# Gate and up projections by seven block products in place of eight, in a decoder block on one core

## The chip, the cores and the metric

The kernel runs on one core of a Trainium2 chip. Its time is the device time of that core in microseconds, as the median of several runs.

## What is computed

One layer of a decoder trunk in float32: a mixer (short convolution, forgetting attention, sliding-window attention, merged by gates), cross attention into 256 memory tokens, a feed-forward, and a last RMSNorm. 512 tokens, 1024 features. The change is in the feed-forward, whose hidden width is 2816, and in what stands around it:

```python
def swiglu(xn, w_gate, w_up, w_down):
    return (jax.nn.silu(xn @ w_gate) * (xn @ w_up)) @ w_down

x = x + cross_attention(rms_norm(x, xattn_norm_g[l]), rms_norm(mem, mem_norm_g[l]), w_xq[l], w_xkv[l], w_xo[l])
x = x + swiglu(rms_norm(x, ffn_norm_g[l]), w_ffn_gate[l], w_ffn_up[l], w_ffn_down[l])
return rms_norm(x, final_norm_g)
```

## The kernel before

Activations lie feature-major, [feature, token]: a product is weights (stationary, 128 x 128) times activations (moving, 512 tokens). Each float32 operand goes to TensorE as a high part, rounded to float32r by ScalarE, and a low part, the difference, from VectorE. A product is then three matmuls (`mm3`: high x high, high x low, low x high), and each matmul loads its own weights.

All weights come as one stream of units of 128 x 1024 numbers (512 KB) in the order of use. `fetch` issues a unit's load on SP's queue into one of three raw buffers (`wr`); `prepare` splits it into one of three `wh` and three `wl` buffers; `next_unit` hands over unit i, having prepared up to i + 2 and asked for loads up to i + 4. `project` runs one unit: eight chunks of features by three matmuls, 24 in all, into a PSUM bank.

The stages near the change, in order:

- *xo*, the output projection of cross attention: for each of eight chunks c a unit of `w_xo`, and then `residual`, which adds the product to x1, splits x1 times the feed-forward's gain into `gx1h` and `gx1l`, and sums the squares for the norm (`add_square`, partly on GpSimd).
- *gate/up*: 22 column blocks j (two units each, one of gate, one of up, products `pfg` and `pfu`). The norm's 1/rms comes after the first two products (`rms_column`, `rms_row`; tiles `ssq_x`, `bc_x`) and is multiplied into both products by VectorE; ScalarE takes the Silu; the product of the two is split at once into `hdh` and `hdl`. Between the blocks 2 to 9, eight groups of four TensorE transposes (`x2T`) turn x1 token-major for the last residual, and ScalarE copies them to `x2t`.
- *down*: token-major, 22 units of `w_d`, eight accumulators (`acc`) of 128 tokens x 512 features. The last four units (`TAIL`) are held back, so that the token blocks finish one after the other and their last norm overlaps with matmuls.

The order of instructions on each engine is set by a scheduler when the program is built, and may differ from the order of the code; each engine then works in its order. A wait is for the last reader or writer of a buffer, by semaphores. Loads on SP's queue are issued in order, so one that waits for its buffer holds back those behind it. Numbers in names of tiles such as `wr119` are the unit's place in the weight stream.

Of the kernel before, what the change touches and what calls it, by code (L numbers as in the profile page):

```python
# [8 lines left out]
F32 = mybir.dt.float32  # L9
F32R = mybir.dt.float32r  # L10
# [6 lines left out]
P = 128  # L17
D = 1024
# [30 lines left out]
def trunk_kernel(ctx: ExitStack, tc: tile.TileContext, a, out: bass.AP):  # L49
    """Activations live feature-major ([feature, token]) so that every product is weights  # L50
    (stationary) x activations (moving); values, and the last projection, come token-major.

    A float32 operand x goes to TensorE as hi = x rounded to float32r and lo = x - hi, which
    is exact, in three one-pass products hi*hi + hi*lo + lo*hi.
    """
# [19 lines left out]
    def split(src, hi, lo, scale=None):  # L75
        """hi + lo = src * scale (scale: a number or one value for each partition)."""
# [9 lines left out]
    # ---------------------------------------------------------------- constants  # L86
# [14 lines left out]
    wlo = pool(ctx, "wlo", bufs=3)  # L101
    stream = []
    order = [("w_a", 25), ("w_g", KC), ("w_o", KC), ("w_k", KC), ("w_q", 2), ("w_v", 4), ("w_q", 6), ("w_v", 4)]
    done = {}
    for name, n in order + [("w_xo", KC), ("w_f", 2 * NF), ("w_d", NF)]:
        t = a[name][done.get(name, 0) :]
        done[name] = done.get(name, 0) + n
        if name == "w_g":
            for c in range(KC):
                stream += [("g", 3 * c + j, t[3 * c + j], 1024) for j in range(3)]  # L110
                stream += [("b", 2 * c + j, a["w_b"][2 * c + j], 768) for j in range(2)]
        else:
            stream += [(name, i, t[i], 1024) for i in range(n)]
    raws, parts = {}, {}
    cursor = [0, 0]

    def fetch(upto):
        while cursor[0] < min(upto, len(stream)):
            i = cursor[0]
            _, _, ap, n = stream[i]  # L120
            raws[i] = wraw.tile([P, 1024], F32, tag="wr", name=f"wr{i}")
            nc.sync.dma_start(raws[i][:, :n], ap)
            cursor[0] += 1

    def prepare(upto):
        while cursor[1] < min(upto, len(stream) - TAIL):
            i = cursor[1]
            n = stream[i][3]
            fetch(i + 1)
            hi = whi.tile([P, 1024], F32R, tag="wh", name=f"wh{i}")  # L130
            lo = wlo.tile([P, 1024], F32R, tag="wl", name=f"wl{i}")
            split(raws.pop(i)[:, :n], hi[:, :n], lo[:, :n])
# [5 lines left out]
    def next_unit(kind):  # L138
        i = used[0]
        assert stream[i][0] == kind, (stream[i][:2], kind)  # L140
# [17 lines left out]
    # two banks for products, in every phase  # L158
# [5 lines left out]
    def rms_column(acc, nblk, sb, name):  # L164
        """acc: squares summed over the chunks, [P, tokens] -> 1/rms as [token, block]."""
# [13 lines left out]
        # one Newton step, as the square root comes from a table  # L179
# [6 lines left out]
    def rms_row(rstd, nblk, sb, name, row=None):  # L186
        """[token, block] -> [P, tokens], the same on every partition."""
# [28 lines left out]
    # ================================================================ mixer  # L216
    x1, gxh, gxl = None, None, None

    def residual(ps, c, acc, g):
        nc.vector.tensor_tensor(x1[:, c, :], x1[:, c, :], ps, op=ALU.add)  # L220
        split(x1[:, c, :], gxh[:, c, :], gxl[:, c, :], gains[:, g, c : c + 1])
# [4 lines left out]
    with yo, mixer:  # L226
        # x times the norm's gain; 1/rms is multiplied in after the products
# [6 lines left out]
        with ExitStack() as attn:  # L234
# [42 lines left out]
            # -------- x, its norm, and [fox v | swa v | forget logits], token-major  # L277
            with ExitStack() as first:
# [22 lines left out]
                # keeps TensorE's clock up until the first loads are there  # L301
# [738 lines left out]
```

## Time and profile before

| | us |
|---|---|
| median of 3 runs | 1046.54 |
| the runs | 1046.53 to 1048.02 |
| span of the profiled execution | 1044.6 |
| TensorE busy | 1032.5 |
| VectorE busy | 547.5 |
| ScalarE busy | 401.6 |
| GpSimd busy | 62.5 |

The profiled execution has no time of its own beside its span: the result gives one time per run, and the span is 1.9 us under their median, for what lies ahead of the first instruction and behind the last. A group's row has line, engine, operation, output<-inputs, shapes and count, then busy time and mean ns of one, then the idle time ahead of them and what ended it. A recorded matmul's duration reaches from its start to its last result, so consecutive matmuls overlap, and their rate is read from their starts.

### The profile page before, as it was taken

To read this page: it belongs to the slowest core of one execution; us is meant where nothing else is said; L and a number is where in the kernel's file an instruction comes from. 1 tells how busy PE (TensorE), PEld (TensorE's weight loads), DVE (VectorE), ACT (ScalarE), POOL (GpSimd) and SP (SyncE) were. 2 spreads that over 40 slices of the span, in tenths; PEclk is the share of its full clock that TensorE was granted. 3 is DMA by queue.
4 is the path that set the end of the run, shared out by engine and by line. 5 is a ranking of instruction groups with operands and counts; after the bars stand their busy time and mean duration, and the time that the engine had idled before them with its cause. 6 is when DMAs were issued, how large, how long until landed. Compare 5 with 4: busy or idle time off the path is not lost.

```text
span 1044.6 us, 12547 instructions
## 1 busy us (share of the span) xinstructions
PE 1032.5 (99%) x4936; PEld 838.1 (80%) x4936; DVE 547.5 (52%) x915; ACT 401.6 (38%) x688; POOL 62.5 (6%) x62
## 2 busy tenths in 40 slices
PE   8999999999999999999999999999999999999997
PEld 6877777878888888888988888888888888888886
DVE  6557767677744444465746554454444444431224
ACT  6445454445522222354534443343333233221124
POOL 5100000001000000033100002200000000000000
PEclk9999999999999999999999999999999999999999
DMA  7431111112222322253442223222223323323222
GB/s 259 144 109 61 61 61 60 62 61 71 91 91 94 100 99 91 91 202 101 141 141 82 81 81 100 90 92 84 98 98 104 100 82 101 99 83 101 93 69 80
DMA packets 30363, 102.20 MB, mean 98 GB/s; under 512 B 3763, under 2 KB 4027, under 8 KB 30177
## 3 DMA queue, kind: packets, MB, share of 16 engines
q1 hardware_dynamic: 27648, 93.37, 27.2%
q0 software_dynamic: 1936, 6.98, 2.2%
q10 hardware_dynamic: 720, 1.07, 0.3%
q8 instruction: 38, 0.62, 0.2%
q14 instruction: 21, 0.16, 0.0%
HBM read 99.29 MB, written 3.68 MB: 99 GB/s over the span
## 4 chain that ended last, share of the span: by engine, by line
PE 97%; DMA 1%; DVE 1%; ACT 1%; issue 1%; SPq 0%; DVEq 0%; ACTq 0%
PE pg L71 4%; PE pg L73 4%; PE pg L72 4%; PE pfg L71 4%; PE pfg L73 4%; PE pfu L72 4%; PE pfu L73 4%; PE pfu L71 4%; PE pfg L72 4%; PE acc L71 4%; PE acc L73 4%; PE acc L72 4%; PE pc L71 2%; PE pbr L73 2%; PE pbr L72 2%; PE pbr L71 2%
## 5 line engine op out<-in xcount | busy, mean ns | idle before, releaser
L78 ACT CAST wh<-wr 128x1024 fp32r<-128x1024 f32 (+1 forms) x167 | 172.3, 1032 | 440.3 <-issue 129.9
L79 DVE TENSOR_TENSOR wl<-wr,wh 128x1024 fp32r<-128x1024 f32 (+1 forms) x167 | 200.0, 1199 | 104.0 <-ACT wh L78 103.3
L71 PE MATMUL pg<-hh,wh 128*128 128x512 f32 x192 | 76.3, 397 | 0.0
L73 PE MATMUL pg<-hh,wl 128*128 128x512 f32 x192 | 75.9, 395 | 0.0
L72 PE MATMUL pg<-hl,wh 128*128 128x512 f32 x192 | 75.9, 395 | 0.0
L71 PE MATMUL pfg<-gx1h,wh 128*128 128x512 f32 x176 | 70.4, 400 | 0.0
L71 PE MATMUL pfu<-gx1h,wh 128*128 128x512 f32 x176 | 69.6, 395 | 0.0
L72 PE MATMUL pfu<-gx1l,wh 128*128 128x512 f32 x176 | 69.6, 395 | 0.0
L73 PE MATMUL pfg<-gx1h,wl 128*128 128x512 f32 x176 | 69.6, 395 | 0.0
L72 PE MATMUL pfg<-gx1l,wh 128*128 128x512 f32 x176 | 69.6, 395 | 0.0
L73 PE MATMUL pfu<-gx1h,wl 128*128 128x512 f32 x176 | 69.6, 395 | 0.0
L73 PE MATMUL acc<-wh,hdl 128*128 128x512 f32 x144 | 57.1, 396 | 0.0
L72 PE MATMUL acc<-wl,hdh 128*128 128x512 f32 x144 | 57.1, 396 | 0.0
L71 PE MATMUL acc<-wh,hdh 128*128 128x512 f32 x144 | 57.1, 396 | 0.0
L640 DVE TENSOR_TENSOR g<-pg,rows 128x512 f32<-128x512 f32 x24 | 16.5, 689 | 76.2 <-PE pg L73 76.2
L841 DVE TENSOR_TENSOR tu<-pfu,row_x 128x512 f32<-128x512 f32 x22 | 15.2, 690 | 70.3 <-PE pfu L73 70.3
L211 POOL TENSOR_TENSOR acc_x<-acc_x,sq_acc_x 128x512 f32<-128x512 f32 x21 | 36.1, 1721 | 182.1 <-ACT sq_acc_x L210 181.7
L839 DVE TENSOR_TENSOR tg<-pfg,row_x 128x512 f32<-128x512 f32 x22 | 15.2, 690 | 53.9 <-PE pfg L73 51.1
L73 PEld LDWEIGHTS pg<-hh,wl 128*128 128x128 f32 x192 | 36.1, 188 | 8.7
L71 PEld LDWEIGHTS pg<-hh,wh 128*128 128x128 f32 x192 | 36.1, 188 | 8.5
L72 PEld LDWEIGHTS pg<-hl,wh 128*128 128x128 f32 x192 | 36.1, 188 | 8.4
L71 PE MATMUL pc<-hh,wh 128*128 128x512 f32 x96 | 41.6, 434 | 0.0
(390 smaller groups left out, 2325.7 us busy)
## 6 DMA issues: line engine op xcount, KB each, us to landing
wr<-in_w_f SPq DMA_DIRECT2D x44, 512.0 KB, 3.4
wr<-in_w_a SPq DMA_DIRECT2D x25, 512.0 KB, 3.5
wr<-in_w_g SPq DMA_DIRECT2D x24, 512.0 KB, 3.4
wr<-in_w_d SPq DMA_DIRECT2D x22, 512.0 KB, 3.4
wr<-in_w_b SPq DMA_DIRECT2D x16, 384.0 KB, 3.0
wr<-in_w_o SPq DMA_DIRECT2D x8, 512.0 KB, 3.5
wr<-in_w_k SPq DMA_DIRECT2D x8, 512.0 KB, 3.5
wr<-in_w_q SPq DMA_DIRECT2D x8, 512.0 KB, 3.4
```

Source lines behind the costliest of these rows:

```text
L71: nc.tensor.matmul(o, wh, xh, start=first, stop=False, **kw)
L72: nc.tensor.matmul(o, wh, xl, start=False, stop=False, **kw)
L73: nc.tensor.matmul(o, wl, xh, start=False, stop=last, **kw)
L78: nc.scalar.copy(hi, src)
L79: nc.vector.tensor_tensor(lo, src, f32(hi), op=ALU.subtract)
L211: nc.gpsimd.tensor_tensor(acc[:, :n], acc[:, :n], sq[:, :n], op=ALU.add)
L640: nc.vector.tensor_tensor(g, pg, row0, op=ALU.mult)
L839: nc.vector.tensor_tensor(tg, pg, row2, op=ALU.mult)
L841: nc.vector.tensor_tensor(tu, pu, row2, op=ALU.mult)
```

## The change

The feed-forward's gate and up weights are cut into blocks: for a pair of column blocks (n = 0, 1) and the even and odd chunks of features (e = 0, 1) the units a11, a12, a21, a22, each with four chunks of gate and four of up. The activations are cut into even and odd chunks and two halves of 256 tokens. A two-by-two block product takes eight block products; here seven are made, of sums of blocks (Winograd's form). Each product is one unit: 2 (gate, up) x 4 chunks x 3 = 24 matmuls of 256 columns. There are 11 pairs, so 77 products.

The seven units of a pair, in order, are a11; a21 + a22; the sum of the two before; a12; a21 + a11; the sum of the third and fourth; a22. Of the four sums, two are made by loading one block and adding the other over it with an accumulating DMA on GpSimd's queue (buffers `ws`, two), and two by VectorE (buffers `wt`, two). The sums of activations (`b1`, `b2`, `bt`) are made in the xo stage. Products gather in three PSUM tiles per pair (`pz`, `px`, `py`), and ScalarE and VectorE copy and combine them into `c1` and `c2`, from which come the gated activations `hd`, unsplit. 1/rms is multiplied into gate alone; the up side's is applied to the last additions, per token. The split of `hd` moves to the down stage (`hidden`), two units ahead of use. The transposes of x1 stand between gate/up and down.

```diff
+            for c in range(n):
+                a11, a12, a21, a22 = (t[4 * c + j] for j in range(4))
+                stream += [
+                    (name, a11, 1024),
+                    (name, (a21, a22), 1024),
+                    (name, (-1, -2), 1024),
+                    (name, a12, 1024),
+                    (name, (a21, a11), 1024),
+                    (name, (-3, -2), 1024),
+                    (name, a22, 1024),
+                ]
...
     def fetch(upto):
...
+            if not isinstance(ap, tuple):
+                if held_by["wr"] == 3:
+                    return
+                raws[i] = wraw.tile([P, 1024], F32, tag="wr", name=f"wr{i}")
+                nc.sync.dma_start(raws[i][:, :n], ap)
+                held_by["wr"] += 1
+            elif not is_local(ap):
+                if held_by["ws"] == 2:
+                    return
+                raws[i] = wsum[0].tile([P, 1024], F32, tag="ws", name=f"ws{i}")
+                nc.sync.dma_start(raws[i], ap[0])
+                nc.gpsimd.dma_start(raws[i], ap[1], accum_op=ALU.add)
+                held_by["ws"] += 1
...
     def prepare(upto):
...
+            if is_local(ap):
+                raws[i] = wsum[0].tile([P, 1024], F32, tag="wt", name=f"wt{i}")
+                nc.vector.tensor_tensor(raws[i], read(i + ap[0]), read(i + ap[1]), op=ALU.add)
...
     def next_unit(kind):
...
         prepare(i + 3)
-        fetch(i + 5)
+        fetch(i + (7 if kind == "w_f" else 5))
...
-        split(x1[:, c, :], gxh[:, c, :], gxl[:, c, :], gains[:, g, c : c + 1])
...
+            nc.scalar.activation(flat, x1[:, c, :], AF.Copy, scale=gains[:, G_FFN, c : c + 1])
+            if e == 0:
+                nc.vector.tensor_tensor(tt[:, 0, :], gx[:, 0, 0, :], gx[:, 0, 1, :], op=ALU.subtract)
+                split(gx[:, 0, 0, :], b1[0][:, q, 0, :], b1[1][:, q, 0, :], -1.0)
+                split(tt[:, 0, :], bt[0][:, q, 0, :], bt[1][:, q, 0, :])
+            else:
+                nc.vector.tensor_tensor(tt[:, 1, :], gx[:, 1, 1, :], tt[:, 0, :], op=ALU.add)
+                split(tt[:, 1, :], bt[0][:, q, 1, :], bt[1][:, q, 1, :])
+                nc.vector.tensor_tensor(tt[:, 2, :], gx[:, 0, 1, :], gx[:, 1, 1, :], op=ALU.subtract)
+                nc.vector.tensor_tensor(tt[:, 3, :], gx[:, 1, 0, :], tt[:, 1, :], op=ALU.subtract)
+                split(gx[:, 1], b2[0][:, q], b2[1][:, q])
+                split(tt[:, 2:4, :], bt[0][:, q, 2:4, :], bt[1][:, q, 2:4, :])
...
-            project(pg, "w_f", gxh, gxl)
-            project(pu, "w_f", gxh, gxl)
...
+        def product(ps, x, j, first):
+
+            wh, wl = next_unit("w_f")
+            for u in range(2):
+                o = ps[:, u * H : (u + 1) * H]
+                for q in range(KC // 2):
+                    w = slice((4 * u + q) * P, (4 * u + q + 1) * P)
+                    mm3(
+                        o, wh[:, w], wl[:, w], x[0][:, q, j, :], x[1][:, q, j, :],
+                        first and u == 0 and q == 0, q == KC // 2 - 1, skip=True,
+                    )
...
+            product(pz, b1, 0, True)
+            nc.scalar.copy(c1[:, 0], gu(pz))
+            product(px, bt, 0, True)
+            nc.scalar.copy(m5, gu(px))
+            product(pz, bt, 1, False)
+            nc.scalar.copy(c1[:, 1], gu(pz))
...
+            product(py, b2, 0, True)
+            nc.vector.tensor_tensor(c1[:, 0], gu(py), c1[:, 0], op=ALU.subtract)
+            product(pz, bt, 2, False)
+            nc.scalar.copy(c2[:, 1], gu(pz))
+            nc.vector.tensor_tensor(c2[:, 1], c2[:, 1], m5, op=ALU.subtract)
+            product(px, b2, 1, False)
+            nc.vector.tensor_tensor(c1[:, 1], gu(px), c1[:, 1], op=ALU.subtract)
+            product(pz, bt, 3, False)
+            nc.scalar.copy(c2[:, 0], gu(pz))
+            for n, cc in enumerate((c1, c2)):
...
+                nc.vector.tensor_tensor(cc[:, :, 0, :], cc[:, :, 0, :], r, op=ALU.mult)
+                nc.scalar.activation(cc[:, :, 0, :], cc[:, :, 0, :], AF.Silu)
+
+                nc.vector.tensor_tensor(h, cc[:, :, 1, :], cc[:, :, 0, :], op=ALU.mult)
...
+        def hidden(f):
...
+            split(hd[:, f, :], hh, hl)
...
             wh, wl = next_unit("w_d")
+            if f + 2 < NF - TAIL:
+                hidden(f + 2)
...
-                nc.vector.tensor_tensor(zt[:, c], o, base, op=ALU.add)
+                nc.vector.scalar_tensor_tensor(
+                    zt[:, c], o, r2[:, t : t + 1], base, op0=ALU.mult, op1=ALU.add
+                )
```

VectorE before, in the middle of gate/up (`tg`, `tu` are gate and up times 1/rms, `hdl` the low part of the gated product); one column block of the feed-forward is six rows:

```order
L841 TENSOR_TENSOR tu13_6880<-pfu13_6818,row_x2_5919 128x512
L842 TENSOR_TENSOR tu13_6880<-tu13_6880,tg13_6879 128x512
L79 TENSOR_TENSOR wl135_6890<-wr135_6823,wh135_6889 128x1024
L79 TENSOR_TENSOR hdl_5816<-tu13_6880,hdh_5815 128x512
L839 TENSOR_TENSOR tg14_6949<-pfg14_6887,row_x2_5919 128x512
L79 TENSOR_TENSOR wl136_6920<-wr136_6853,wh136_6919 128x1024
```

VectorE in the changed kernel, from the second pair (units 112 to 118) towards the third (119 to 125); `wl116` and `wl117` are the low parts of the second pair's fifth and sixth units, `ws120` is the third pair's first accumulated sum:

```order
L195 TENSOR_TENSOR wt121_6398<-ws120_6234,wr119_6203 128x1024
L90 TENSOR_TENSOR wl116_6231<-ws116_6097,wh116_6230 128x1024
L90 TENSOR_TENSOR wl117_6265<-wt117_6262,wh117_6264 128x1024
L195 TENSOR_TENSOR wt124_6494<-wt121_6398,wr122_6297 128x1024
L953 TENSOR_TENSOR c1_1_6163<-py1_6162,c1_1_6163 128x512
L90 TENSOR_TENSOR wl118_6294<-wr118_6172,wh118_6293 128x1024
L90 TENSOR_TENSOR wl119_6326<-wr119_6203,wh119_6325 128x1024
L956 TENSOR_TENSOR c2_1_6164<-c2_1_6164,m5_1_6165 128x512
L958 TENSOR_TENSOR c1_1_6163<-px1_6161,c1_1_6163 128x512
L964 TENSOR_TENSOR c1_1_6163<-c1_1_6163,row_x2_6028 128x2x256
L90 TENSOR_TENSOR wl120_6358<-ws120_6234,wh120_6357 128x1024
```

The scheduler has moved the third pair's sums `wt121` and `wt124` ahead of the second pair's fifth and seventh low parts (`wl116`, `wl118`).

SP's queue of loads before, in gate/up, one plain load per unit:

```order
L122 DMA wr114_6035<-in_w_f 128x1024
L122 DMA wr115_6081<-in_w_f 128x1024
L122 DMA wr116_6111<-in_w_f 128x1024
L122 DMA wr117_6157<-in_w_f 128x1024
L122 DMA wr118_6187<-in_w_f 128x1024
```

SP's queue in the changed kernel, the third pair's loads; for each `ws` an accumulating DMA (`L171`) of the same size stands in GpSimd's queue, which waits until the plain load has landed:

```order
L164 DMA wr119_6203<-in_w_f 128x1024
L170 DMA ws120_6234<-in_w_f 128x1024
L164 DMA wr122_6297<-in_w_f 128x1024
L170 DMA ws123_6329<-in_w_f 128x1024
L164 DMA wr125_6404<-in_w_f 128x1024
```

Five loads on SP and two on GpSimd take the place of four on SP per pair of column blocks; the load of `ws120` waits for the last reader of `ws113`, which is its low part `wl113`.

ScalarE before, where gate/up ends and down begins (`hdh` is the high part of the last gated product, `wh151` on are units of `w_d`):

```order
L840 ACTIVATE tg21_7439<-tg21_7439 128x512
L78 CAST wh151_7470<-wr151_7383 128x1024
L78 CAST hdh_5815<-tu21_7440 128x512
L78 CAST wh152_7500<-wr152_7413 128x1024
L78 CAST wh153_7530<-wr153_7474 128x1024
```

ScalarE in the changed kernel at the same place, from the copy of the last product; `hh0` is the high part of the first unit's hidden activations, `hh18` to `hh20` those of the tail:

```order
L960 COPY c2_10_8252<-pz10_8248 128x512
L89 CAST hh18_9166<-hd_5886 128x512
L89 CAST hh19_9174<-hd_5886 128x512
L981 COPY x2t_8487<-x2T00_8491 128x512
L965 ACTIVATE c2_10_8252<-c2_10_8252 128x2x256
L981 COPY x2t_8487<-x2T01_8497 128x512
L981 COPY x2t_8487<-x2T10_8503 128x512
L89 CAST hh20_9182<-hd_5886 128x512
L981 COPY x2t_8487<-x2T11_8509 128x512
L981 COPY x2t_8487<-x2T20_8515 128x512
L89 CAST hh0_8562<-hd_5886 128x512
```

The copies of the transposes and three high parts of the tail now stand between the last product's copy and the first high part that the down stage needs.

More of the change, by code (lines that the diff above doesn't have):

```diff
@@ L104, in trunk_kernel @@
     done = {}
-    for name, n in order + [("w_xo", KC), ("w_f", 2 * NF), ("w_d", NF)]:
+    for name, n in order + [("w_xo", KC), ("w_f", NF // 2), ("w_d", NF)]:
         t = a[name][done.get(name, 0) :]
@@ L119, in fetch, with read @@
             i = cursor[0]
-            _, _, ap, n = stream[i]
-            raws[i] = wraw.tile([P, 1024], F32, tag="wr", name=f"wr{i}")
-            nc.sync.dma_start(raws[i][:, :n], ap)
-            cursor[0] += 1
+            _, ap, n = stream[i]
+            if not isinstance(ap, tuple):
[11 more added lines that the diff above has]
+                held_by["ws"] += 1
+            cursor[0] += 1
+    def read(i):
+        readers[i] -= 1
+        if readers[i]:
+            return raws[i]
+        _, ap, _ = stream[i]
+        if not isinstance(ap, tuple):
+            held_by["wr"] -= 1
+        elif not is_local(ap):
+            held_by["ws"] -= 1
+        return raws.pop(i)
     def prepare(upto):
@@ L812, in trunk_kernel @@
         second_half(3)
-        acc2 = small.tile([P, S], F32, tag="acc", name="acc_x2")
+    acc2 = small.tile([P, S], F32, tag="acc", name="acc_x2")
+    ff = ExitStack()
+    bp = pool(ff, "ffb")
+    H = S // 2
+    b1, b2, bt = (
+        [bp.tile([P, KC // 2, n, H], F32R, name=f"b{t}{x}") for x in "hl"] for t, n in (("1", 1), ("2", 2), ("t", 4))
+    )
+    wsum.append(pool(ff, "wsum", bufs=2))
+    with xo, ExitStack() as pj:
+        g2 = pool(pj, "gpair", bufs=2)
+        gx = None
         for c in range(KC):
@@ L847, in trunk_kernel @@
+    x2p = pool(xs, "x2t")
+    x2t = x2p.tile([P, NB, D], F32, name="x2t")
+    with ExitStack() as tr:
+        pT = pool(tr, "pT4", bufs=2, space=PSUM)
+        for t in range(NB):
+            for e in range(2):
                 tp = pT.tile([P, 512], F32, tag="T", name=f"x2T{t}{e}")
@@ L865, in trunk_kernel, with down @@
         tail_w = []
-        def down(o, t, c, f, wh, wl, first=0, last=NF - 1):
+        def down(o, t, c, f, hh, hl, wh, wl, first=0, last=NF - 1):
             tok = slice(t * P, (t + 1) * P)
-            mm3(o, hdh[:, f, tok], hdl[:, f, tok], wh[:, c], wl[:, c], f == first, f == last)
+            mm3(o, hh[:, tok], hl[:, tok], wh[:, c], wl[:, c], f == first, f == last)
+        hs = {}
+        def hidden(f):
+            sb, tag = (f3, "") if f < NF - TAIL else (tl, f"{f}")
+            hh = sb.tile([P, S], F32R, tag=f"hh{tag}", name=f"hh{f}")
+            hl = sb.tile([P, S], F32R, tag=f"hl{tag}", name=f"hl{f}")
+            split(hd[:, f, :], hh, hl)
+            hs[f] = hh, hl
         halves = [slice(e * 512, (e + 1) * 512) for e in range(2)]
+        hidden(0)
+        hidden(1)
         for f in range(NF - TAIL):
             wh, wl = next_unit("w_d")
+            if f + 2 < NF - TAIL:
+                hidden(f + 2)
             for t in range(NB):
@@ L876, in trunk_kernel @@
                     last = NF - TAIL - 1 if (t, e) == (NB - 1, 1) else NF - 1
-                    down(acc[t, e], t, c, f, wh, wl, last=last)
+                    down(acc[t, e], t, c, f, *hs[f], wh, wl, last=last)
         for f in range(NF - TAIL, NF):
@@ L883, in trunk_kernel @@
             lo = tl.tile([P, 1024], F32R, name=f"twl{f}")
-            split(raws.pop(i), hi, lo)
+            split(read(i), hi, lo)
             cursor[1] += 1
-            tail_w.append((f, hi, lo))
+            hidden(f)
+            tail_w.append((f, *hs[f], hi, lo))
         zl = tl.tile([P, 512], F32, name="zl")
-        nc.vector.tensor_tensor(zl, acc[NB - 1, 1], x2t[:, NB - 1, 512:], op=ALU.add)
+        nc.vector.scalar_tensor_tensor(
+            zl, acc[NB - 1, 1], r2[:, NB - 1 : NB], x2t[:, NB - 1, 512:], op0=ALU.mult, op1=ALU.add
+        )
         for t in range(NB):
@@ L901, in trunk_kernel @@
             for n, (c, o, base, first) in enumerate(parts_):
[L902 to L904 removed]
+                for f, hh, hl, wh, wl in tail_w:
+                    down(o, t, c, f, hh, hl, wh, wl, first)
+                nc.vector.scalar_tensor_tensor(
+                    zt[:, c], o, r2[:, t : t + 1], base, op0=ALU.mult, op1=ALU.add
+                )
                 nc.scalar.activation(zg[:, c], zt[:, c], AF.Square, accum_out=ss[:, n : n + 1])
@@ L992, in _layout @@
     o["w_xo"] = blocks(g["w_xo"][0], range(0, D, P))
-    wg = blocks(g["w_ffn_gate"][0], range(0, FF, P))
-    wu = blocks(g["w_ffn_up"][0], range(0, FF, P))
-    o["w_f"] = np.stack([wg, wu], axis=1).reshape(2 * NF, P, 1024)
+    gu = [g[f"w_ffn_{n}"][0].reshape(4, 2, P, NF // 2, 2, P) for n in ("gate", "up")]
+    o["w_f"] = np.ascontiguousarray(np.stack(gu).transpose(4, 5, 2, 3, 0, 1, 6)).reshape(2 * NF, P, 1024)
     o["w_d"] = g["w_ffn_down"][0].reshape(NF, P, D)
```

85 lines of the change are left out of this document (48 added, 37 removed).

## The prediction

> **What bounds the kernel now.** I read the page first (busy shares, then the chain of waits), then the table by stage, then single tiles of the stages that the change touches.
>
> ```profile
> span 1044.6 us, 12547 instructions
> PE 1032.5 (99%) x4936; PEld 838.1 (80%) x4936; DVE 547.5 (52%) x915; ACT 401.6 (38%) x688; POOL 62.5 (6%) x62
> ...
> PE 97%; DMA 1%; DVE 1%; ACT 1%; issue 1%; SPq 0%; DVEq 0%; ACTq 0%
> ```
>
> TensorE is busy 99% of the span and 97% of the chain that ended last: the kernel takes as long as its matmuls take to issue. The other engines follow it. The stages behind the sum, in the table by stage (busy time of each engine, granted clock, DMA share, GB/s):
>
> ```profile
> core 0: us, PE busy (x) PEld busy (x) DVE busy (x) ACT busy (x) POOL busy (x), PEclk, DMA share, GB/s
> 500.00:525.00 25.00, 25.00 (x212) 24.54 (x211) 18.10 (x33) 12.38 (x19) 2.04 (x2) 1.00 0.49 165
> 671.00:914.00 243.00, 243.00 (x1066) 196.20 (x1066) 108.36 (x137) 76.41 (x97) 0.55 (x1) 1.00 0.29 95
> ```
>
> The second row is gate/up before: TensorE never pauses, at a clock of 1.00, with VectorE under half busy. The first row is the keys' projection of cross attention, whose matmuls have 256 columns: the nearest thing in this trace to the new products.
>
> **What a matmul costs.** Their recorded durations overlap, so I count from starts. Tile and timeline rows (duration min/median/max, first and last start), and three lines of the chain:
>
> ```profile
> L71 PE MATMUL pfg<-gx1h,wh x176: 391/394/483, 663.4 to 908.3; 128*128 128x512 f32 x176
> 674.71 0.44 PE ssq_x L169 x4
> 680.05 0.84 PE bc_x L196 x8
> 698.43 0.44 PE x2T L849 x4
> 914.57 0.39 PE L71 MATMUL acc<-wh,hdh 128*128 128x512 f32 x1
> ```
>
> From the first gate matmul at 663.4 to the first matmul of the down stage at 914.57 are 251.2 us. Less the norm (0.44 + 0.84 = 1.3) and eight groups of transposes (8 x 0.44 = 3.5), 246.4 us are left for 22 x 48 = 1056 matmuls: 233 ns each, 22.4 us for the 96 of two column blocks.
>
> ```profile
> L71 PE MATMUL pk<-gmh,wh x64: 276/276/366, 502.2 to 525.1; 128*128 128x256 f32 x64
> 513.28 0.44 PE ssq_x L169 x4
> 521.90 0.84 PE bc_x L196 x8
> 525.46 0.39 PE L71 MATMUL pq<-gx1h,wh 128*128 128x512 f32 x1
> 1035.37 0.28 PE L71 MATMUL last<-twh,hdh 128*128 128x256 f32 x1
> 1037.16 0.28 PE L71 MATMUL last<-twh,hdh 128*128 128x256 f32 x1
> ```
>
> The keys: 525.46 - 502.2 - 1.3 = 22.0 us for 192 matmuls, 114 ns each. The last tile of the kernel: five groups of three between the two starts, 1.79 / 15 = 119 ns. I take 116.5, half of 233, with 114 and 119 as ends. So a 256-column matmul costs half a 512-column one, new weights for each included.
>
> **Part 1, the products.** Seven products of 2 x 4 x 3 = 24 matmuls for a pair of blocks: 168 instead of 192 halves, 168 x 0.1165 = 19.6 us instead of 22.4. Over 11 pairs 1848 x 0.1165 = 215.3 us instead of 246.4: **-31.1 us** (-26.5 to -35.7), if the weights come in time.
>
> **Part 2, the work beside it.** The rows that price it:
>
> ```profile
> L79 DVE TENSOR_TENSOR wl<-wr,wh 128x1024 fp32r<-128x1024 f32 x151 | 184.7, 1224 | 104.0 <-ACT wh L78 103.3
> L841 DVE TENSOR_TENSOR tu<-pfu,row_x 128x512 f32<-128x512 f32 x22 | 15.2, 690 | 70.3 <-PE pfu L73 70.3
> L711 DVE TENSOR_TENSOR kt<-pk,rowm 128x256 f32<-128x256 f32 x8 | 3.4, 424 | 1.8 <-PE pk L73 1.1
> L78 ACT CAST wh<-wr 128x1024 fp32r<-128x1024 f32 x151 | 158.9, 1053 | 389.9 <-issue 129.9 <-PE pfg L72 72.3 <-PE acc L73 66.5
> L840 ACT ACTIVATE tg<-tg 128x512 f32<-128x512 f32 x22 | 13.8, 626 | 0.1
> L78 ACT CAST hdh<-tu 128x512 fp32r<-128x512 f32 x22 | 13.7, 623 | 9.9 <-DVE tu L842 9.9
> L852 ACT COPY x2t<-x2T 128x512 f32<-128x512 f32 x8 | 4.6, 581 | 0.0
> ```
>
> VectorE, per pair: seven low parts and two sums of weights at 1.22, three combinations and four multiplications at 0.69: 9 x 1.22 + 7 x 0.69 = 15.9 us of 19.6. ScalarE: 7 x 1.05 + 4 x 0.58 + 2 x 0.63 = 10.9. DMA: seven transfers of 512 KB in 19.6 us, 187 GB/s, against 165 carried without a pause in the keys' stage. On average none is the bound. The new sums of activations in the xo stage add, for two chunks of 2 x 24 x 0.233 = 11.2 us, seven VectorE operations of 256 columns and two of 512 in place of the two old low parts: 7 x 0.42 + 2 x 0.69 + two residuals 1.4 + two weights 2.4 = 8.1 us, inside the 11.2, so I charge nothing. The last chunk's first result is due 48 x 0.1165 = 5.6 us after the last pxo matmul, for a chain of residual, scaled copy, sum, high and low part (0.69 + 0.72 + 0.42 + 0.4 + 0.42 = 2.7; the copy's 0.72 is what x2's old scaled copy took, its half-width cast about 0.4): covered. If that cover went, some 3 us would come once.
>
> **Part 3, the wait that is added.** The accumulating load. In VectorE's new queue the local sum for the *next* pair (`wt121`) stands ahead of the low parts of this pair's fifth and sixth units (`wl116`, `wl117`). VectorE works in order, so if `ws120` isn't complete, TensorE stops before the fifth product. And `ws120` can't be loaded early: its buffer holds `ws113`, free only when `wl113` is done. That makes a ring, once per pair: `wl113` done, plain load into the buffer, accumulating load over it, local sum, low part of unit five, two products, then (`L958`, `L964` ahead of it in the queue) `wl120`. Its rows:
>
> ```profile
> wr<-in_w_f SPq DMA_DIRECT2D x44, 512.0 KB, 3.4
> x<-in_xT POOLq DMA_DIRECT2D x4, 512.0 KB, 5.7
> gf<-in_final_g POOLq DMA_DIRECT2D x1, 512.0 KB, 4.0
> DMA to landing us min/median/max: 4.1/5.7/7.7
> GB/s 340 321 19 0 0 0 0 0 101 334 347 25 32 95 397 277 32 145 372 277 13 151 302 340 13 113 246 372 76 0 38 145 416 208 101 271 397 38 38 183
> ```
>
> Load 3.4; accumulate A; sum 1.22; low part 1.22; 48 matmuls 5.6, and 0.16 until the last one's result is there (276 ns of duration less 117); combination 0.69, multiplication 0.69, low part 1.22. That is 14.2 + A, and six hand-overs between engines at about 0.1 (my estimate): **ring = A + 14.8**. A pair takes the longer of the ring and 19.6, so the accumulate is hidden up to A = 4.8.
>
> No accumulating DMA is in this trace. Its lower end: a plain 512 KB load from the same queue, alone, takes 4.0 (`gf`). Nothing lets it be less, since it moves the same bytes and reads the destination too. The upper end of the rows is 7.7, the last of four loads of x that ran together (fourth row: their least, median and greatest). The GB/s row (40 slices of the keys' stage) peaks at 416, so 512 KB take 1.26 us of data at least. The destination's bytes are a second read, +1.26, giving 5.3; and one plain load of 512 KB (`wr122`, queued right behind `ws120`) falls into the accumulate, of which I take half. **A = 6.0**, near the median of the loads that shared the engines. The Trainium skill, Collectives: The Full Stack (the section on the bandwidth ceiling, the fold count and why AG, RS and AR differ), says that an add in the DMA is slow because of its two source reads, which halve the rate, and not because of the adding. By that rule alone, without the other load, A would be near 5.3, and the sum some 6 us lower than mine; no run here shows it yet.
>
> With A = 6.0 the ring is 20.8, 1.2 us over the products. It bites in nine pairs (the first pair's sums, and the second's first, are fetched during the xo stage; the last has no successor): 9 x 20.8 + 2 x 19.6 + 1.3 = 227.7 us from the first product to the last.
>
> **Part 4, the change of stage.** Before, the down stage began without a pause (914.57 follows gate/up directly). Now ScalarE, after the last product, does in order the copy, two high parts of the tail, an x2 copy, the Silu, two x2 copies, a high part, two x2 copies, and only then `hh0`, which the first down matmul needs: 0.16 + 0.58 + 1.25 + 0.58 + 0.63 + 1.16 + 0.62 + 1.16 + 0.62 = 6.8, with hand-overs 7.0 us. Seven of the eight groups of transposes lie in it and the eighth (0.4) behind: **7.4 us** where the transposes alone took 3.5. In the down stage a high part of 0.62 and a low part of 0.69 are added per 5.6 us unit on engines with more than half free: nothing. The scaled last additions cost 0.06 more each, the last one 0.1 with its wait. The gain's load now stands behind 22 accumulates in POOL's queue, 100 us before use: nothing.
>
> **The sum.** Before: 251.2. After: 227.7 + 7.4 = 235.1. Difference -16.1; with 0.1 of the end -16.0. Against the profiled execution's own time, span 1044.6 and some 1.9 us around it to the median of 1046.5: **1030.5 us**.
>
> **Rivals.**
>
> *The accumulate is hidden (A up to 4.8).* For it: the same queue's plain load takes 4.0. Against: two reads, and another load in the way. Then 11 x 19.6 + 1.3 + 7.4 = 224.3, -26.9: **1020**; with 114 ns 1015.
>
> *The accumulate is slow and the kernel is slower.* Place: VectorE's `wt` sums, at `L195`, waiting for the POOL queue's DMA, TensorE idle before each fifth product. It decides where 9 (A + 14.8) + 39.2 + 1.3 + 7.4 = 251.2, at A = 7.8, a tenth above the slowest 512 KB load of that queue. At A = 10, 9 x 24.8 + 47.9 = 271.1, +19.9: **1066**. For it: nothing in the trace bounds the adding from above. Against: the median of 5.7 under load.
>
> *The pauses lower the clock.* One more row of the table by stage, from the first loads:
>
> ```profile
> 10.00:21.00 11.00, 9.03 (x57) 8.27 (x56) 9.30 (x8) 10.37 (x18) 6.07 (x5) 1.00 0.87 284
> ```
>
> There TensorE idled 2 us of 11 and the granted clock stayed 1.00, which speaks against; at A = 6 it idles 1.2 us in one piece per pair of 20.8, but near A = 7.8 three. If the two products of the ring ran at half speed, nine rings would be 5.6 longer: 1030 + 50 = **1081**. The Trainium skill, TensorE: Matmul & The Clock Gate (the section on the HAM clock gate), halves the clock after an idle window of about 3.4 us; by that rule the forecast's pauses are too short.
>
> That the change doesn't do what it says is out: the new queue of TensorE holds 1848 matmuls of 256 columns for 1056 of 512.
>
> **How the numbers follow.** A difference under 0.2% (2.1 us) can't be told from none. Forecast (A from 4.8 to 7.6): 0.48. Hidden: 0.24. Slow accumulate: 0.20. Lower clock: 0.04. Within 0.2% of before (A about 7.6 to 8.0): 0.04. So faster 0.72, same 0.04, slower 0.24. The forecast's own range is 1020 to 1044. The range for 8 in 10, 1016 to 1060, cuts the hidden case below 116 ns (some 6 in 100) and the slow one above A = 9.3 with the lower clock (13 in 100).
>
> **What the changed profile would show.** Part 1: starts of pz, px, py 114 to 119 ns apart inside a product. Part 3: the accumulating issue landing after 5 to 7.6 us; VectorE idle at the `wt` sum until that DMA; one pause of TensorE per pair, before the fifth product, of about 1.2 us. Part 4: 7 us from the last pz matmul to the first of the down stage. The forecast is wrong if the accumulates take under 4.8 or over 7.8 us, or if 256-column matmuls with fresh weights don't keep 119 ns for 200 us, which the trace shows for 23 us only.

## The result, and the profile after

The changed kernel takes **1059.5 us** (median of 4 runs, 1055.0 to 1063.5) against 1046.5: ratio 1.012, 95% interval 1.009 to 1.015. It is slower; the forecast was 1030.5. Its profiled execution took 1058.8 us, near the median.

From the page of the changed kernel (span, busy time of each engine, granted clock in 40 slices, DMA groups with the median time from issue to landing):

```profile
span 1057.0 us, 14492 instructions
PE 1012.7 (96%) x5728; PEld 866.7 (82%) x5728; DVE 639.6 (61%) x1009; ACT 471.7 (45%) x796; POOL 81.2 (8%) x84
...
PEclk8999999999999999999999999998998989999999
...
wr<-in_w_f SPq DMA_DIRECT2D x33, 512.0 KB, 4.2
...
ws<-in_w_f SPq DMA_DIRECT2D x22, 512.0 KB, 3.8
ws<-in_w_f POOLq DMA_DIRECT2D x22, 512.0 KB, 7.2
```

TensorE is no longer busy 99% of the span, and the granted clock, 1.00 throughout gate/up before, dips in slices 28, 31 and 33, which lie in gate/up. The accumulating load (last row) takes a median of 7.2 us. The table by stage, first gate/up with the change of stage, then the down stage:

```profile
core 0: us, PE busy (x) PEld busy (x) DVE busy (x) ACT busy (x) POOL busy (x), PEclk, DMA share, GB/s
665.58:930.38 264.80, 233.18 (x1890) 229.84 (x1888) 172.17 (x195) 131.43 (x174) 19.39 (x22) 0.94 0.58 150
930.38:1057.00 126.62, 120.60 (x546) 100.20 (x544) 49.55 (x65) 42.02 (x67) 0.00 (x0) 1.00 0.25 84
```

Gate/up takes 264.8 us where it took 251.2. One turn of the ring, from issue to the matmul that waits (timeline rows of SP's queue, POOL, VectorE and TensorE: start, duration, instruction; brackets: idle time ahead and its releaser), and how long the two loads in it took (tile view of each, one load alone):

```profile
782.77 0.33 SPq L170 DMA_DIRECT2D ws<-in_w_f  x1
788.40 0.86 POOL L171 DMA_DIRECT2D ws<-in_w_f  x1 [10.32 <-DVE wl L90]
796.57 1.22 DVE L195 TENSOR_TENSOR wt<-ws,wr 128x1024 f32<-128x1024 f32 x1 [8.09 <-issue]
798.98 0.58 PE L84 MATMUL pz<-bth,wl 128*128 128x256 f32 x1 [5.00 <-DVE wl L90]
```

```profile
DMA to landing us min/median/max: 5.1/5.1/5.1
...
DMA to landing us min/median/max: 8.1/8.1/8.1
```

The plain load lands at 787.8, the accumulating one at 796.5, and the sum of the *next* pair starts 0.1 us later; it stands ahead of the low part that the fifth product needs, and TensorE has waited 5.0 us. ("issue" as the releaser is the landing of that DMA: it ended 0.1 us before, after POOL's issuing instruction had long been done.) So it goes nearly once per pair (chain of waits, us in total, times, longest):

```profile
PE pz L84 <- DVE wl L90: 28.7, 9, 5.0
```

The clock in two pauses and behind them (table by stage; ahead of the pause, in it, behind it, later):

```profile
716.00:719.60 3.60, 3.60 (x33) 3.58 (x31) 0.00 (x0) 1.66 (x3) 0.23 (x1) 1.00 0.83 141
719.60:723.20 3.60, 0.19 (x2) 0.00 (x0) 2.38 (x3) 0.92 (x1) 0.00 (x0) 0.80 0.11 22
723.20:728.30 5.10, 5.07 (x23) 5.07 (x24) 4.07 (x4) 0.18 (x1) 0.86 (x1) 0.50 0.31 103
728.30:741.90 13.60, 13.60 (x120) 13.60 (x120) 8.61 (x10) 8.16 (x11) 0.86 (x1) 0.99 0.71 174
793.80:798.90 5.10, 0.18 (x2) 0.00 (x0) 2.33 (x3) 0.92 (x1) 0.00 (x0) 0.80 0.03 6
798.90:803.40 4.50, 4.42 (x20) 4.42 (x21) 4.12 (x5) 0.00 (x0) 0.36 (x1) 0.50 0.36 117
```

Behind each pause of 3.7 us or more (seven of them, from start to start) the matmuls run at half the clock for 3.1 to 5.9 us, some 14 to 27 of them 220 ns apart instead of 113. After the one pause of 1.9 us, at 697.8, they don't.

**Where the 12.4 us of span went**, by starts of matmuls (first product 665.58, last matmul of the last product 923.53, first of the down stage 930.38):

| | before | after | difference |
|---|---|---|---|
| up to the first product | 663.4 | 665.6 | +2.2 |
| products at full clock, 1056 x 233.3 or 1848 x 114.3 ns | 246.4 | 211.2 | -35.2 |
| pauses ahead of a fifth product (8 over 1 us) | 0 | 29.8 | +29.8 |
| half clock behind seven of them | 0 | 14.2 | +14.2 |
| shorter waits | 0 | 1.6 | +1.6 |
| norm, transposes, change of stage | 4.8 | 8.0 | +3.2 |
| down stage and end | 130.0 | 126.6 | -3.4 |

The first row is mostly not the change: 1.4 us of it are there at the first matmul of the xo stage, where the two programs have done the same work (616.2 before, 617.6 after). The expectations below count the two rows of 14.2 and 1.6 us together as half clock, 15.8.

### The profile page after: what moved, and what is told of

It is laid out like the page before. It is cut to its first block, busy times and chain, and to the rows that moved or that the text cites. A ratio compares the mean times of both kernels' runs of the same rounds, so it can differ in the third digit from the quotient of the medians.

```text
span 1057.0 us, 14492 instructions
## 1 busy us (share of the span) xinstructions
PE 1012.7 (96%) x5728; PEld 866.7 (82%) x5728; DVE 639.6 (61%) x1009; ACT 471.7 (45%) x796; POOL 81.2 (8%) x84
## 5 line engine op out<-in xcount | busy, mean ns | idle before, releaser
L84 PE MATMUL pz<-bth,wl 128*128 128x256 f32 x264 | 80.4, 305 | 28.7 <-DVE wl L90 28.7
L84 PEld LDWEIGHTS pz<-bth,wl 128*128 128x128 f32 x264 | 55.7, 211 | 30.5 <-DVE wl L90 30.5
L82 PE MATMUL pz<-bth,wh 128*128 128x256 f32 x264 | 79.0, 299 | 0.0
L83 PE MATMUL pz<-btl,wh 128*128 128x256 f32 x264 | 78.7, 298 | 0.0
L84 PE MATMUL acc<-wh,hl 128*128 128x512 f32 x144 | 56.1, 390 | 0.0
L83 PE MATMUL acc<-wl,hh 128*128 128x512 f32 x144 | 56.0, 389 | 0.0
L82 PE MATMUL acc<-wh,hh 128*128 128x512 f32 x144 | 56.0, 390 | 0.0
L83 PEld LDWEIGHTS pz<-btl,wh 128*128 128x128 f32 x264 | 55.7, 211 | 0.0
L82 PEld LDWEIGHTS pz<-bth,wh 128*128 128x128 f32 x264 | 55.4, 210 | 0.0
L171 POOL DMA_DIRECT2D ws<-in_w_f x22 | 19.0, 862 | 338.6 <-DMA ws<-in_w_f 130.1
```

The costliest lines, as they stand in the source:

```text
L82: nc.tensor.matmul(o, wh, xh, start=first, stop=False, **kw)
L83: nc.tensor.matmul(o, wh, xl, start=False, stop=False, **kw)
L84: nc.tensor.matmul(o, wl, xh, start=False, stop=last, **kw)
L171: nc.gpsimd.dma_start(raws[i], ap[1], accum_op=ALU.add)
```

## The experiments

Each ran beside the kernel before on the same chip: numbers 1 to 4 on one, 5 to 9 on another, where the kernel before took 1046.5 and 1046.7 us. T is the theory that the ring through the accumulating load makes the pauses, and the pauses the half clock.

**1. No accumulating load** (T against "VectorE doesn't keep pace with shorter products").

```diff
                 nc.sync.dma_start(raws[i], ap[0])
-                nc.gpsimd.dma_start(raws[i], ap[1], accum_op=ALU.add)
```

> The accumulating load is left out, so two of the four weight sums of each pair consist of one block only; every other instruction stays. In the profile of the changed kernel the products take 1848 x 114.3 ns = 211 us, TensorE's pauses before the fifth products 29.8 us, and the half-speed stretches behind them 15.8 us more. Theory (the ring with a late accumulate): without the accumulate the ring is 14.8 plus 1 to 2 us for the slower plain load, under the 19.2 us of the seven products, so pauses and half speed both go: 1059.5 - 45 = about 1014 us, clock 1.00 throughout. Rival (the work beside the products, VectorE above all, does not keep pace with products of 256 columns): pauses stay and the time stays above 1040.

Measured: 1018.3 us (1010.7 to 1019.0), ratio 0.971, 0.968 to 0.975. Groups by line and the table by stage, between 700 and 850 us, of this kernel:

```profile
L84 PE MATMUL pz<-bth,wl 128*128 128x256 f32 x264 | 73.0, 276 | 0.0
700.00:850.00 150.00, 150.00 (x1326) 150.00 (x1326) 118.88 (x128) 85.89 (x110) 0.00 (x0) 1.00 0.46 140
```

No pause and full clock: TensorE issues without a break while VectorE carries 119 us of work in 150. Part 2 of the prediction holds, and the rival falls. T expected 1014; the profiled run took 1010.7, the other three 8 us more, which is taken up below.

**2. The second load overwrites instead of adding** (is it the add, or the queue and the loads beside it?).

```diff
-                nc.gpsimd.dma_start(raws[i], ap[1], accum_op=ALU.add)
+                nc.gpsimd.dma_start(raws[i], ap[1])
```

> The second load of each sum comes from the same queue, at the same place and with the same bytes, but overwrites instead of adding, so two of the four sums of each pair consist of one block only. If the add makes the transfer slow (two reads): landing 4 to 5 us instead of a median of 7.2, ring 16.5 + 4.5 = 21, pauses of about 1.8 us, perhaps without a fall of the clock: 1014 + 9 x 1.8 = about 1030 us. If the second transfer of POOL's queue is slow for another reason (the queue, the other loads beside it): landing stays near 7 us and the time near 1055.

Measured: 1024.7 us (1021.9 to 1027.1), ratio 0.979, 0.977 to 0.981. DMA groups of this kernel; then, from its timeline, two starts after a pause, six turns of the ring apart:

```profile
ws<-in_w_f SPq DMA_DIRECT2D x22, 512.0 KB, 4.1
ws<-in_w_f POOLq DMA_DIRECT2D x22, 512.0 KB, 4.8
```

```profile
738.32 0.39 PE L84 MATMUL pz<-bth,wl 128*128 128x256 f32 x1 [1.32 <-DVE wl L90]
863.07 0.39 PE L84 MATMUL pz<-bth,wl 128*128 128x256 f32 x1 [1.24 <-DVE wl L90]
```

Same queue, place and bytes: a median of 4.8 us without the add, 7.2 with it. The ring is (863.07 - 738.32) / 6 = 20.79 us. In these six turns its own plain loads took 4.46 us and its second loads 4.97 on average, so the rest of it is 11.36 us, which is what the prediction gave it (14.8 less the plain load's 3.4); the plain load was taken 1.1 us too short. Pauses of 1.0 to 2.5 us remain, and behind them the clock stays up. The table by stage, right behind the longest of them:

```profile
821.90:825.00 3.10, 3.09 (x27) 3.09 (x28) 3.07 (x4) 0.38 (x1) 0.00 (x0) 1.00 0.49 169
```

**3. TensorE kept busy in the pauses** (is the half clock a cost of its own?).

```diff
+            if 2 <= i <= 9:
+                wm = bank(f"warm{i}")
+                for _ in range(12):
+                    nc.tensor.matmul(wm, idle[:, :P], idle, start=True, stop=True)
             product(pz, bt, 2, False)
```

> In pairs 2 to 9, twelve matmuls of zeros (512 bf16 columns, some 2.6 us together) stand ahead of the fifth product, so that TensorE works through most of its pause; nothing waits for their result. Theory that the pauses also lower the clock and that this lengthens the ring: the clock stays 1.00, the two products behind the pause lose their 2 us each, the ring falls from 24.4 to 22.4, and the time to about 1059.5 - 16 = 1043 us. Rival (the half-speed stretches only fill time in which the ring would have waited anyway, or the clock falls for another reason): 1059 us.

Measured: 1049.7 us (1046.8 to 1052.8, 10 runs), ratio 1.003, 1.002 to 1.004. From the timeline of this kernel, the starts behind the first and the last filled pause, seven turns apart; its table by stage, between 700 and 850 us and behind a pause that is not filled; and the changed kernel's own starts, eight turns apart:

```profile
725.78 0.39 PE L84 MATMUL pz<-bth,wl 128*128 128x256 f32 x1 [1.09 <-DVE wl L90]
889.85 0.38 PE L84 MATMUL pz<-bth,wl 128*128 128x256 f32 x1 [1.61 <-DVE wl L90]
```

```profile
700.00:850.00 150.00, 141.00 (x1140) 132.04 (x1147) 97.41 (x106) 68.41 (x88) 11.16 (x13) 0.99 0.58 155
700.50:705.10 4.60, 4.59 (x26) 4.59 (x27) 4.05 (x4) 0.68 (x1) 0.54 (x1) 0.63 0.35 114
```

```profile
699.74 0.39 PE L84 MATMUL pz<-bth,wl 128*128 128x256 f32 x1 [1.63 <-DVE wl L90]
894.92 0.39 PE L84 MATMUL pz<-bth,wl 128*128 128x256 f32 x1 [3.73 <-DVE wl L90]
```

The clock stays at 0.99 where it was 0.91, and the ring falls from (894.92 - 699.74) / 8 = 24.4 us to (889.85 - 725.78) / 7 = 23.4. The second row is the control within this run: the pause up to 700.5, 3.7 us long and not filled, is followed by half clock as before. The half clock has a price of its own: 9.8 us in the medians. That is less than the 16 expected, since a turn gave back 1.0 us and not 2.0: the half clock lengthens a turn by 1.4 (table below), and this kernel's own loads in the ring took 0.4 us longer.

**4. Four buffers for the loaded sums, their loads issued earlier** (break the ring, keep every instruction).

```diff
+WS = 4
...
-                if held_by["ws"] == 2:
-                    return
-                raws[i] = wsum[0].tile([P, 1024], F32, tag="ws", name=f"ws{i}")
...
+    def load_sums(upto):
+        while ahead[0] < min(upto, len(stream)):
...
+                if not wsum or held_by["ws"] == WS:
+                    return
+                raws[i] = wsum[0].tile([P, 1024], F32, tag="ws", bufs=WS, name=f"ws{i}")
...
         fetch(i + (7 if kind == "w_f" else 5))
+        if kind in ("w_xo", "w_f"):
+            load_sums(i + 14)
```

> Four buffers instead of two for the loaded sums, and their two loads are issued up to 14 units ahead instead of 7, apart from the order of the other loads; what is computed is the same. Theory (ring): no local sum waits for an accumulate any more, since it lands a whole pair early, so the pauses go and with them the half speed: 1012 to 1018 us, faster than both kernels. Rival (the DMA itself cannot carry seven transfers and two second reads in 19.2 us beside each other): accumulates land later still, pauses stay in part, 1030 to 1050.

Measured: 1020.1 us (1016.0 to 1021.8), ratio 0.974, 0.971 to 0.977: faster than both kernels. A second profile of the same kernel ran in 1012.5. The group of products that had waited, in the first profile, then in the second; and the accumulating load of the second:

```profile
L85 PE MATMUL pz<-bth,wl 128*128 128x256 f32 x264 | 74.3, 281 | 0.0
```

```profile
L85 PE MATMUL pz<-bth,wl 128*128 128x256 f32 x264 | 73.0, 277 | 0.4 <-DVE wl L91 0.4
```

```profile
ws<-in_w_f POOLq DMA_DIRECT2D x22, 512.0 KB, 7.2
```

The accumulate still takes 7.2 us; it just lands before anybody needs it. So its length costs nothing off the ring, and the DMA does carry the load: this rival falls too. The number of buffers and the earlier issue were changed together, so which of the two is needed isn't shown.

**5. The local sums kept in program order on VectorE**, two buffers as before (is it the place in VectorE's queue?).

```diff
-                nc.vector.tensor_tensor(raws[i], read(i + ap[0]), read(i + ap[1]), op=ALU.add)
+                tc.keep_in_program_order(
+                    nc.vector.tensor_tensor(raws[i], read(i + ap[0]), read(i + ap[1]), op=ALU.add)
+                )
```

> One thing is changed: each local sum of weights is kept in program order on VectorE, so that the sum for the next pair stands behind the low parts of this pair's fifth and sixth units instead of ahead of them. Buffers, loads and accumulates stay; what is computed is the same. Theory (ring through the order of VectorE's queue): no product of this pair waits for the next pair's accumulate any more. What is left as a ring, once per pair, is plain load 4, accumulate 7.2, hand-overs 1, two sums and low parts 3, some 15 us, under 19.2. So the pauses go: 1010 to 1020 us, as with four buffers. Rival (two buffers are too few whatever the order): pauses move to another product of the pair, 1035 to 1055.

Measured: 1027.8 us (1024.7 to 1029.0), ratio 0.982, 0.980 to 0.983. TensorE no longer waits ahead of the fifth product, but the time is 8 to 15 above that of four buffers. The accumulating load of one sum and how long it took; then ScalarE, VectorE and TensorE at the start of the pair that uses it:

```profile
798.49 0.86 POOL L171 DMA_DIRECT2D ws<-in_w_f  x1 [15.87 <-DMA ws<-in_w_f]
...
DMA to landing us min/median/max: 9.2/9.2/9.2
...
807.79 1.05 ACT L89 CAST wh<-ws 128x1024 fp32r<-128x1024 f32 x1 [2.75 <-DVE c L966]
812.61 1.22 DVE L196 TENSOR_TENSOR wt<-ws,wr 128x1024 f32<-128x1024 f32 x1
813.87 1.05 ACT L89 CAST wh<-wt 128x1024 fp32r<-128x1024 f32 x1 [1.42 <-DVE wt L196]
814.94 1.23 DVE L90 TENSOR_TENSOR wl<-wt,wh 128x1024 fp32r<-128x1024 f32 x1 [1.11 <-ACT wh L89]
814.96 0.39 PE L82 MATMUL pz<-bth,wh 128*128 128x256 f32 x1 [0.55 <-ACT wh L89]
```

Now the sum is made just in time, its high part behind it, its low part behind that: a chain of 3.5 us in which the third product waits, with more of the same in the products after it. And the accumulate is still waited for, at another place: it lands at 807.7 (798.49 + 9.2), and 0.1 us later ScalarE, idle for 2.75 us, casts the sum. The last pair's gating stands behind this cast, and the local sum behind the gating. In each of the nine pairs from the third on the cast starts 0.1 us after the landing, ScalarE having idled 1.3 to 4.2 us (the profile names now one instruction, now another as what ended this wait; the lag behind the landing is always the same), and the next load into the buffer is issued 0.5 us after the local sum has ended. So the ring is closed again, at 20.3 us a turn (692.00 to 854.49, eight turns, by issues of the first sum's plain load), where the 168 matmuls of a pair take 19.0 at 113.3 ns.

Starts more than 130 ns apart cost 16.8 us in gate/up beyond their 114 ns each (51 of them, 22.66 us together), where the first profile of four buffers has 3.0. So the place in VectorE's queue is what carried the accumulate's lateness to the fifth product, and with it a longer ring; but the rival is right that with two buffers a wait remains at other products, only it is smaller than priced. My expectation had accumulates of 7.2 us, where two that run at once take 7.9 to 10.4, and 3 us behind them, where 6.6 to 7.3 pass from the landing to the next load's issue. Whether the late place costs anything with four buffers, no run shows.

**6. On top of 5: the first hidden parts made inside gate/up, half of the residual's copies on VectorE** (the fourth part of the prediction).

```diff
+            if i in (7, 8):
+                f = i - 7
...
+                split(hd[:, f, :], hh, hl)
...
-                nc.scalar.copy(x2t[:, t, e * 512 : (e + 1) * 512], tp)
+                (nc.scalar.copy if e else nc.vector.tensor_copy)(x2t[:, t, e * 512 : (e + 1) * 512], tp)
```

> On top of the order of the first kernel: high and low parts of the first two hidden blocks are made inside gate/up (two buffers for them), and half of the eight copies of the transposed residual go from ScalarE to VectorE; what is computed is the same. If the 6.9 us between the last product and the first matmul of the down stage are ScalarE's queue, as in the prediction's fourth part: 3.5 to 4.5 us instead of 6.9, so about 3 us less than the first kernel. Rival (the transposes themselves or the last pair's results set it): no difference.

Measured: 1029.9 us (1029.0 to 1031.3), 2 more than number 5 instead of 3 less. The step itself does what it should: the first down matmul follows the last product at once (last pz matmul at 891.25; timeline).

```profile
891.37 0.39 PE L82 MATMUL acc<-wh,hh 128*128 128x512 f32 x1
...
893.08 1.09 PE L988 MATMUL x2T<-ident,x 128*128 128x128 f32 x8
```

The transposes now stand among the down matmuls and wait twice for the copy of an earlier one, and a down matmul waits once (0.6 to 0.7 us each); hidden parts have two buffers here in place of three. The down matmuls start 234.2 ns apart for 100 us where number 5 has 226.7: 426 x 7.5 ns = 3.2 us more. From the last product to the end the kernel takes 136.0 us (1027.3 - 891.3), number 5 133.5: without the spacing some 0.7 us are gained and not 3. The removed wait is shown; what it is worth stays open.

**7. Two short pauses in the kernel before** (what sets that spacing?).

```diff
+            if j == 0:
+                zb = f2.tile([P, P], BF16, tag="zb", name="zb0")
+                nc.scalar.copy(zb, po[:, :P])
+                nc.tensor.matmul(pg, zb, idle, start=True, stop=True)
...
+        nc.scalar.copy(zb, pu[:, :P])
...
+        nc.tensor.matmul(acc[0, 0], zb, idle, start=True, stop=True)
```

> The kernel before, with two short pauses of TensorE added: ahead of the first gate product and ahead of the first matmul of the down stage stands one matmul of zeros whose weights ScalarE first copies from the result just finished (about 1 us each); the result of it is overwritten. Asked: in all kernels with a pause between gate/up and the down stage the down matmuls start 226.7 ns apart, in the kernel before 234.3. If a pause sets the spacing: 528 x 7.6 ns = -4.0 us in the down stage, up to 1056 x 6.7 = -7 us in gate/up, +2 for the pauses: 1037 to 1044 us. If the spacing belongs to what the matmuls read: +2, 1048 to 1049 us.

Measured: 1049.6 us (1049.5 to 1051.3), ratio 1.003, 1.002 to 1.004. The pauses are there, and the down matmuls behind the second are still 234.2 ns apart. That a pause always brings the closer spacing is wrong.

**8, 9. Second profiles of numbers 1 and 4**, for the spread of their runs.

> The same kernel as the one without the accumulating load (two of the four sums of each pair consist of one block only), for a second profile. Its runs lay at 1010.7 once and at 1018.0 to 1019.0 three times; the profiled one was the fast one, with products 113.3 ns apart. Theory (a kernel's matmuls can settle into one of two spacings, and that is the spread of its runs): a run near 1018.5 shows 117.8 ns in all of gate/up, 1848 x 4.45 = 8.2 us more; one near 1010.7 shows 113.3. Rival (the spread comes from pauses): 113.3 ns and pauses that add up to 8 us.

> The same kernel as the one with four buffers, for a second profile. Its runs lay at 1016.0 to 1021.8, the profiled one at 1019.6 with 117.8 ns. By the theory of two spacings: either 117.8 ns again near 1020, or 113.3 ns near 1012, or a mixture between; no pause over 1.3 us after the first pair in any case. By the rival, the spacing is the kernel's own: 117.8 ns again whatever the time.

Measured: 1011.8 us for number 1, with 113.3 ns again, so a run near 1018 wasn't caught; 1012.5 for number 4, with 113.3 ns in gate/up except between 808.7 and 817.6 us, where it has 117.8. Its first profile, taken on the other chip, had 117.8 from 678 us to the end of gate/up and took 1019.6. The table by stage over the same 200 us of gate/up, first and second profile:

```profile
680.00:880.00 200.00, 200.00 (x1700) 200.00 (x1699) 149.90 (x160) 111.73 (x143) 13.74 (x16) 1.00 0.61 167
```

```profile
680.00:880.00 200.00, 198.02 (x1742) 197.54 (x1740) 154.25 (x167) 116.03 (x150) 14.31 (x17) 1.00 0.64 176
```

The same program, the same clock, no pause over 0.8 us in either: 1700 matmuls or 1742. So the spacing isn't the kernel's own, and that rival falls; nor is it the chip's, since one execution shows both. From first to last product they take 220.1 and 213.2 us, 6.9 of the 7.1 between the two spans.

## Why the prediction was wrong

**Part 1 held.** Products at full clock start 114.3 ns apart (116.5 taken, 114 the lower end): 4.1 us better than forecast.

**Part 2 held.** Without the accumulate VectorE keeps pace (experiment 1). In the xo stage the products begin 0.8 us later than the stage's start alone explains, but that is the spacing of this stage's own matmuls, 233.3 ns where it was 228.9 (192 x 4.4 ns = 0.8 us); the new work there costs nothing, as charged.

**Part 3 is the step that failed: right place, wrong size.** TensorE pauses before each fifth product, behind a `wt` sum that waits for the POOL queue's DMA, as said. But the ring is 24.4 us a turn, not 20.8. The medians of the page are over all loads of the kernel; the terms of the ring are those of its own loads, the first sum of each pair, averaged here over the turns between the starts shown above:

| term of the ring | taken | changed kernel | experiment 2, no add | experiment 3, pauses filled |
|---|---|---|---|---|
| plain load | 3.4 | 5.0 | 4.5 | 5.6 |
| second load (accumulate A) | 6.0 | 6.6 | 5.0 | 6.4 |
| half clock behind the pause | none | 1.4 | none | none |
| everything else | 11.4 | 11.4 | 11.4 | 11.4 |
| ring, by starts | 20.8 | 24.4 | 20.8 | 23.4 |

"Everything else" came out as predicted: wherever the clock stayed up it is 8.3 us from the waiting matmul to the issue of the next plain load, 0.6 from that load's landing to the accumulate's issue, and 2.5 from the accumulate's landing to the waiting matmul. (The row of the half clock is what the 8.3 grew by behind the pauses.) Three terms were too small: the plain load by 1.6 us, A by 0.6, and the half clock, put at nothing, by 1.4.

The plain load was the largest miss. Its 3.4 came from the kernel before, where no accumulate runs. From the changed kernel, the accumulate of a pair's second sum and how long it took, then the ring's plain load beside it, then the ring's plain load of the one later turn in which that accumulate was done:

```profile
703.66 0.85 POOL L171 DMA_DIRECT2D ws<-in_w_f  x1 [11.76 <-DMA ws<-in_w_f]
...
DMA to landing us min/median/max: 9.3/9.3/9.3
...
708.04 0.33 SPq L170 DMA_DIRECT2D ws<-in_w_f  x1
...
DMA to landing us min/median/max: 6.8/6.8/6.8
...
859.90 0.33 SPq L170 DMA_DIRECT2D ws<-in_w_f  x1
...
DMA to landing us min/median/max: 3.6/3.6/3.6
```

Seven of the nine plain loads of the ring, from 686.94 on, were issued 1.6 to 4.9 us before the other sum's accumulate had landed, and took 4.2 to 6.8 us; the other two (686.94, 2.5 us after that landing, and 859.90, 0.1 us before it) took 3.6. Without any accumulate (experiment 1) the loads of the sums took 3.4 to 4.5. The prediction put half of a plain load into A and nothing of the other accumulate into the plain load.

The second read of A was about right: the shortest accumulate lands in 5.3 us in the changed kernel and in 5.2 in experiment 4. The Trainium skill, Collectives: The Full Stack (the section on the bandwidth ceiling, the fold count and why AG, RS and AR differ), puts the cost of the add in a ReduceScatter down to its two source reads; the estimate from it, 5.3, agrees with these shortest ones, and experiment 2's 2.4 us between overwriting and adding, in the medians, has the same sign.

**The rivals.** "Slow accumulate" is what came, at the place that it named, but not by its price: it asked for A = 7.8, and the ring's accumulates took 6.6. That alone would have left the forecast at 1030.5 + 9 x 0.6 = some 1036 us, faster than before. The plain load of 5.0 makes it 1030.5 + 9 x 2.2 = some 1050 (both are estimates from the table above); experiment 3, the ring with hardly any half clock, took 1049.7, nearer than such a sum can claim. The half clock brings the other 10 of the 13 us. The sign that the prediction had set, accumulates over 7.8 us, did not come in the median (7.2): the largest miss lay in a term without a sign.

"The pauses lower the clock", given 0.04, was no case of its own but what follows once the ring is late enough: the turn up to 723.24, all of its matmuls at full clock, took 23.5 us and ended in a pause of 3.7. I had written that near A = 7.8 it is three, and priced neither case with the other. Its price of 5.6 us a ring was too high; 14 to 27 matmuls behind a pause ran at half clock, not 48, and a turn grew by 1.4. The Trainium skill, TensorE: Matmul & The Clock Gate (the section on HAM oscillation), describes this pattern, a wait for a DMA in each turn that is longer than the gate's window of about 3.4 us and a cold start behind it; the trace agrees: pauses of 3.7 us and more were followed by half clock, those up to 2.5 us (experiment 2) were not. The nearest to the edge is one of 3.5 us in experiment 3 (747.4 to 751.0, also from start to start), with the clock at 1.00 behind it.

"Hidden" would have needed A = 4.8; with the add taken out the ring's second loads take 5.0, and TensorE still pauses 1.0 to 2.5 us a turn.

**Part 4 held:** 923.64 to 930.38 are 6.7 us where 7.4 were taken, and ScalarE's queue is the reason: with the first hidden parts made earlier, the wait was gone (experiment 6, which also moved half of the copies to VectorE).

**The down stage**, charged nothing, came out 3.4 us shorter, since its matmuls are 226.7 ns apart and not 234.1: 528 x 7.4 ns = 3.9. Nothing in the prediction foresaw it.

Against the forecast the sum reads: +2.2 at the start, -4.1 products, +19.0 pauses (29.8 for 10.8), +14.2 half clock, +1.6 shorter waits, -0.7 change of stage, -3.5 down stage: +28.7, where the profiled execution lies 28.4 above.

## What to carry to other kernels

A wait that comes once per turn is priced by the whole ring that it closes, each term as it is under the load of that stage: here the doubtful term, the accumulate, was looked at from all sides, and the plain load, carried over from a stage without it, was the larger miss. Where the margin is a third of an uncertain term, both sides of it deserve a price, with what the longer pause sets off behind it (here the half clock, 9.8 us by experiment 3). The remedy was not a faster transfer but more buffers and an earlier issue: with four in place of two the same accumulate, as slow as before, costs nothing, and the seven products bring most of what they promise. To move the waiting instruction later in its queue made the ring shorter, but did not open it: the wait for the same load came out on another engine. So after such a move, look for who now starts right behind the landing.

## What was not expected of the hardware

The same matmuls, at a granted clock of 1.00 and without pauses, start at one of a few spacings: 512 columns 226.7, 229 or 233.3 to 234.2 ns, 256 columns 113.3 or 117.8, for 100 us and more at a time. One program showed both (experiment 4: 1012.5 and 1019.6 us). What chooses isn't settled. Among the products of gate/up the spacing changes only where TensorE has waited, be it by 0.1 us, in either direction (experiment 4's second profile: to 117.8 at 808.7, back to 113.3 behind the wait of 0.7 us that ends at 817.6); most waits leave it as it is, as in experiment 7, and in experiment 6's down stage it changed at 1001 us without one. It is worth up to 8 us here, 1848 x 4.4 ns (6.9 were seen), so differences under 1% between these kernels aren't to be read as their own.
